# Prompt scores as two 128-row products with copied key parts, and half-wide cache tiles, in a two-layer streaming encoder step

## Chip, cores and metric

The kernel runs on one core of one Trainium2 chip. The metric is device time in microseconds (us) of one execution of the whole kernel. Before the change the median of three runs is 3021.28 us (3018.55 to 3021.63).

## What is computed

One step of a two-layer encoder over 1024 new tokens of one stream (the prompt) and 16 new tokens of each of eight running streams (the sample). Layer 0 mixes by stick-breaking attention (8 heads of 64) beside a convolution; layer 1 by banded attention (16 heads of 64) with a learned bias. Each layer ends in an MLP. The scores, which the change touches, are in the reference:

```python
def stick_breaking(q, k, v, q_pos, k_pos):
    z = jnp.einsum('bqhd,bkhd->bhqk', q, k) * (HEAD_DIM ** -0.5)
    mask = k_pos[None, :] < q_pos[:, None]
    log_keep = jnp.where(mask, jax.nn.log_sigmoid(-z), 0.0)
    between = lax.cumsum(log_keep, axis=3, reverse=True) - log_keep
    w = jnp.where(mask, jnp.exp(jax.nn.log_sigmoid(z) + between), 0.0)
    return jnp.einsum('bhqk,bkhd->bqhd', w, v)

def band_attention(q, k, v, q_pos, k_pos, rel_bias):
    s = jnp.einsum('bqhd,bkhd->bhqk', q, k) * (HEAD_DIM ** -0.5)
    ...
    p = jax.nn.softmax(jnp.where(mask, s, -jnp.inf), axis=-1)
    return jnp.einsum('bhqk,bkhd->bqhd', p, v)
```

## The kernel before

All dense products are made on TensorE in a reduced float32 type (F32R). To keep accuracy, a float32 operand is split into a high part (a copy in F32R, by ScalarE) and a low part (the rest, by VectorE), and a product takes three matmuls: high by high, high by low, low by high (`SPLIT`, L34; `split`, L173; `dense`, L205).

Activations lie transposed, features on the 128 partitions and tokens along the free axis. Heads go in pairs `p`: the head dimension is 64, so head 0 of a pair lies on partitions 0 to 63 and head 1 on 64 to 127. Layer 0 (`mixer0`, L544) has 4 pairs, layer 1 (`mixer1`, L991) has 8. For each pair the work is: projections of q, k and v of the *next* pair (`proj`, as filling), the spread of q and k into matmul operands (`expand_qk`), the scores of 8 query tiles of 128 per head (`attend`), stick-breaking or softmax on ScalarE and VectorE, transposes and the product with v (`weigh_steps`), and the sample's attention against cached keys and values (`sample_steps`).

How a score is made before the change:

- Layer 0: `qh`, `ql`, `kh`, `kl` are one tile each for both heads. A score block of up to 512 keys takes three matmuls on 64 rows (L820), and the last block of a query tile a fourth one on 128 rows that adds the mask (L822, `unit` by `maskd`).
- Layer 1: `qs` holds, for each head, the high part of q on the head's own 64 partitions and the low part on the other 64. `kd` holds the high part of k on both halves; the second half is filled by a copy DMA from SBUF to SBUF on the POOL queue (L1035). So one 128-row matmul gives (high + low of q) by high of k (L1101). The low part `kl` of k stands on the head's own partitions alone, and the second matmul is one of 64 rows (L1102). A query tile has one block up to 512 keys, and two (384 and 256) from the fifth tile on.

VectorE also makes the convolution of layer 0 (`tap`, L608): 31 multiply-adds over 1024 tokens for each of 4 channel groups, dealt out over the stages by `level` and `TAPS`. The sample's caches come through `load` in `sample_caches` (L423): tiles `ct` of 2048 columns (1 MB), two buffers, the next tile asked for when one is used. The DMAs for caches and weights stand on one queue (SP), and its wait for a free buffer holds back what is behind it.

The order of the work is set in three steps. `merge` (L50) deals lists of steps into one by their estimated TensorE time and the lags between dependent steps; `level` (L76) deals the taps among them; and the tile framework then fixes a static order for each engine, which may move an instruction past others. Engines wait for each other by semaphores and each works through its own queue in order.

Of the kernel before, what the change touches and what calls it, by code (L numbers as in the profile page):

```python
# [8 lines left out]
F32 = mybir.dt.float32  # L9
F32R = mybir.dt.float32r  # L10
# [27 lines left out]
def f(ap):  # L38
    return ap.bitcast(F32)
# [77 lines left out]
def tile_trunk(ctx, tc, ins, outs):  # L117
# [8 lines left out]
    def pool(name):  # L126
        return tc.tile_pool(name=name, bufs=1, reuse_waits="tile")
# [181 lines left out]


    class Cat:

# [92 lines left out]
    def sample_caches(layer, p, pl):  # L405


        name = f"{layer}{p}"
        srcs = {}
        for bg in range(2):  # L410
            if layer == 0:
                for c in range(2):
                    srcs["k", bg, c] = ins["sb_k"][p, bg * 4:bg * 4 + 4, :, c * 512:(c + 1) * 512]
            else:
                srcs["k", bg, 0] = ins["band_k"][p, bg * 2:bg * 2 + 2]
        for bg in range(2):
            for c in range(2 if layer == 0 else 1):
                srcs["v", bg, c] = ins["sb_v" if layer == 0 else "band_v"][p, bg, :, c * 2048:(c + 1) * 2048]
        order = list(srcs)
        at = {k: n for n, k in enumerate(order)}  # L420
        got = {}

        def load(kind, bg, n):  # L423
            i = at[kind, bg, n]
            for key in order[i:i + 2]:
                if key not in got:
                    got[key] = pl.tile([P, 2048], F32, tag="ct", name=f"ct{name}{key[0]}{key[1]}{key[2]}")
                    src = srcs[key]
                    if key[0] == "k":
                        src = src.rearrange("b p k -> p b k")  # L430
                        dma(got[key].rearrange("p (b k) -> p b k", b=src.shape[1]), src)
                    else:
                        dma(got[key], src)
            return got[kind, bg, n]

        return load

    def sample_steps(layer, p, bg, s, wk, load, soft, cs):

        nz = 2 if layer == 0 else 1
        name = f"{layer}{p}{bg}"
        qb = s["qb"]
# [8 lines left out]
        def keys(c):  # L453
            if c == 0:
                box["z"] = [bank(f"zs{name}{e}") for e in range(nz)]
            k = load("k", bg, c)
            for b in range(4):
                own = slice(32 * b, 32 * b + 32)
                mm(box["z"][c][own], qb[:, own], k[:, b * 512:b * 512 + 512], start=True, stop=True)  # L459

# [21 lines left out]
        def prod(k4):  # L482
            if k4 == 0:
                box["o"] = bank(f"so{name}")
                mm(box["o"][:, 0:P], wt["n"], s["vn"], start=True, stop=False)
            v = load("v", bg, k4)
            for j in range(4):
                for b in range(4):
                    own = slice(32 * b, 32 * b + 32)
                    c = j * P + 32 * b  # L490
                    mm(box["o"][own, 0:P], wt[k4][:, c:c + 32], v[:, (4 * j + b) * P:(4 * j + b + 1) * P], start=False,
                       stop=k4 == nz - 1 and j == 3)
# [9 lines left out]
        return ([Step(100.0, queries, 0.0, f"q{name}")]  # L502
                + [Step(1300.0, lambda c=c: keys(c), 0.0, None, f"q{name}", 3000) for c in range(nz)],
                [Step(215.0, new_keys, 2700.0 if layer == 0 else 1600.0, f"new{name}")],
# [39 lines left out]
    def mixer0():  # L544
        with ExitStack() as st:

            ep = Bufs(st.enter_context(pool("early0")), sg=3, kp=2)
            cp = Bufs(st.enter_context(pool("cache0")), ct=2)
            qb = ep.tile([P, P], F32, "qb", "qb0")
# [85 lines left out]
            def start():  # L635
# [21 lines left out]
                def ready(n, half):  # L657
                    src, t = st[n, half]
                    hl = None
                    if n > 1:  # L660
                        tag = ("qh", "ql", "kh", "kl")[2 * n - 4 + half]
# [113 lines left out]
            def expand_qk(p):  # L775
                q, k = S["sq", p], S["sk", p]
                ACT(qh, q[:, :TP], AF.Copy, scale=0.125)
                stt(ql, q[:, :TP], 0.125, f(qh), ALU.mult, ALU.subtract)
# [26 lines left out]
            def attend(p, cat):  # L805
                def job(i, t):
                    ws = {}
                    own = slice(64 * i, 64 * i + 64)

                    def one(q):  # L810
                        n = (q + 1) * P
                        w = ep.tile([P, TP], F32, "sg", f"sg{p}{i}{q}")
                        keep = ep.tile([P, TP + P], F32, "kp", f"kp{p}{i}{q}")
                        qs = slice(q * P, q * P + P)
                        for c in range(0, n, 512):
                            m = min(512, n - c)
                            z = bank(f"z{p}{i}{q}{c}")
                            last = c + m == n
                            for e, (a, b) in enumerate(((qh, kh), (qh, kl), (ql, kh))):
                                mm(z[:, :m], a[own, qs], b[own, c:c + m], start=e == 0, stop=e == 2 and not last)  # L820
                            if last:
                                mm(z[:, m - P:m], unit, maskd, start=False, stop=True)  # L822
# [9 lines left out]
                    def cost(q):  # L832
                        return 3 * max(256, q * P + P) * PASS

# [20 lines left out]
            start()  # L855
            qh, ql, kh, kl = (ep.tile([P, TP], F32R, n, n) for n in ("qh", "ql", "kh", "kl"))
            vs = pp.tile([P, 8, 2, 2, HD], F32R, "vs", "vs0")
# [133 lines left out]
    def mixer1(nx, win):  # L991
        h, rstd = nx.h, nx.r
        with ExitStack() as st:
# [35 lines left out]
            def expand_qk(p):  # L1029
                q, k = S["sq", p], S["sk", p]  # L1030
                for i in range(2):
                    own = slice(64 * i, 64 * i + 64)
                    oth = slice(64 - 64 * i, 128 - 64 * i)
                    ACT(kd[own, i], k[own, :TP], AF.Copy)
                    nc.gpsimd.dma_start(kd[oth, i], kd[own, i])  # L1035
                    ACT(qs[own, i], q[own, :TP], AF.Copy, scale=0.125)
                    stt(qs[oth, i], q[own, :TP], 0.125, f(qs[own, i]), ALU.mult, ALU.subtract)
                    tt(kl[own], k[own, :TP], f(kd[own, i]), ALU.subtract)
# [47 lines left out]
            def attend(p, cat):  # L1086
                def job(i, t):
                    ws = {}
                    own = slice(64 * i, 64 * i + 64)

                    def one(q):
# [6 lines left out]
                        for c, m in ((0, n),) if n <= 512 else ((0, 384), (384, 256)):  # L1098
                            z = bank(f"zc{p}{i}{q}{c}")
                            kc = slice(k0 + c, k0 + c + m)  # L1100
                            mm(z[:, :m], qs[:, i, qc], kd[:, i, kc], start=True, stop=False)  # L1101
                            mm(z[:, :m], qs[own, i, qc], kl[own, kc], start=False, stop=True)  # L1102
                            pieces.append((z[:, :m], S["bp", p, i][:, b0 + c:b0 + c + m], c, m))
# [357 lines left out]
```

## Time and profile before

| | us |
|---|---|
| median of three runs | 3021.28 |
| the profiled execution | 3022.33 |
| its span | 3020.5 |
| TensorE (PE) busy | 2958.1 |
| VectorE (DVE) busy | 2006.0 |
| ScalarE (ACT) busy | 1090.8 |
| mean granted TensorE clock, share of full | 0.987 |

The profile is of one execution. PE is matmuls, PEld loads of their stationary operand, which overlap matmuls. A matmul's recorded duration includes its way through the array, so that durations of neighbours overlap; what one costs in a stream is read from the distance between starts. In shapes such as `64*128 64x512`, the first pair is active rows by columns of the array, the second the moving operand. By time, layer 0's mixer takes some 90 to 600 us of the span, its output projection and MLP go on to about 1450, layer 1's mixer lies at about 1450 to 2135, and the rest is layer 1's output projection and MLP.

### The profile page before, as it was taken

Reading aid. Unit: us, or ns where it says so; the run is one execution under the profiler, and the core shown is the slowest. Engines: PE = TensorE matmul, PEld = TensorE weight load, DVE = VectorE, ACT = ScalarE, POOL = GpSimd, SP = SyncE. Lnnn points to the kernel's source line nnn. Section 1 sums busy time; section 2 is a strip of 40 time slices with the busy share of each in tenths; the row PEclk is TensorE's granted clock in tenths of the full one; section 3 lists DMA queues with packets and bytes.
Section 4 is the critical chain, followed back from the end, with each engine's and each line's share of the span. In section 5 each row is a group of like instructions: output and inputs, shape, how many; then the busy total and the mean of one; then the engine's idle time right before and its main releaser. Section 6 shows DMA issues by size and latency. Waiting matters only on the chain.

```text
span 3020.5 us, 45292 instructions
## 1 busy us (share of the span) xinstructions
PE 2958.1 (98%) x17786; PEld 2780.7 (92%) x17786; DVE 2006.0 (66%) x4021; ACT 1090.8 (36%) x2260; POOL 134.4 (4%) x293
## 2 busy tenths in 40 slices
PE   8999998999999999999999999999999999999998
PEld 8987786899999999999988888887999999999998
DVE  7998997865555555556666666667665555555556
ACT  5344446643222222222445444455442222222223
POOL 1000001000000000000101000100000000000001
PEclk9998998999999999999999999999999999999999
DMA  4333335331111111111433333335411111111101
GB/s 152 111 99 105 121 116 181 124 115 64 35 49 36 49 36 49 36 50 46 137 121 119 113 110 116 118 119 195 163 53 39 46 42 43 43 43 46 39 32 63
DMA packets 106677, 254.74 MB, mean 84 GB/s; under 512 B 17520, under 2 KB 22832, under 8 KB 102368
## 3 DMA queue, kind: packets, MB, share of 16 engines
q1 hardware_dynamic: 91728, 204.87, 20.4%
q0 software_dynamic: 14592, 46.97, 4.8%
q8 instruction: 139, 2.28, 0.3%
q14 instruction: 74, 0.61, 0.1%
q10 hardware_dynamic: 144, 0.02, 0.0%
HBM read 205.71 MB, written 41.84 MB: 82 GB/s over the span
## 4 chain that ended last, share of the span: by engine, by line
PE 85%; DVE 10%; ACT 3%; issue 1%; DMA 1%; DVEq 0%; SPq 0%; ACTq 0%
PE psu L214 26%; PE pd L1217 26%; PE psc L214 10%; PE psob L214 4%; PE psp L214 2%; DVE y L623 2%; PE psoa L214 2%; PE zc L1102 2%; PE avc L362 2%; DVE kp L801 2%; PE tpc L350 2%; PE zc L1101 1%; PE f L214 1%; PE zs L459 1%; PE z L820 1%
## 5 line engine op out<-in xcount | busy, mean ns | idle before, releaser
L214 PE MATMUL psu<-m,hl_wu 128*128 128x384 f32 x4608 | 808.3, 335 | 0.0
L1217 PE MATMUL pd<-hid,hl_wd 128*128 128x384 f32 x4608 | 807.4, 334 | 0.0
L214 PEld LDWEIGHTS psu<-m,hl_wu 128*128 128x128 f32 x4608 | 799.5, 188 | 1.6
L1217 PEld LDWEIGHTS pd<-hid,hl_wd 128*128 128x128 f32 x4608 | 799.5, 188 | 1.1
L1221 DVE TENSOR_TENSOR x<-x,pd 128x384 f32<-128x384 f32 x768 | 415.8, 550 | 194.6 <-PE pd L1217 191.8
L214 PE MATMUL psc<-h,hl_wc 128*128 128x384 f32 x1728 | 344.4, 345 | 0.0
L214 PEld LDWEIGHTS psc<-h,hl_wc 128*128 128x128 f32 x1728 | 293.5, 188 | 21.9 <-issue 15.0
L1201 DVE TENSOR_TENSOR s<-psu,rm 128x384 f32<-128x384 f32 x192 | 106.1, 555 | 282.7 <-PE psu L214 273.8
L175 ACT ACTIVATE hid<-s 128x384 fp32r<-128x384 f32 x192 | 100.7, 527 | 378.7 <-PE pd L1217 332.9
L175 ACT ACTIVATE hl_wd<-st_wd 128x512 fp32r<-128x512 f32 x128 | 80.6, 632 | 333.2 <-DMA st_wd<-in_w_down_dram 230.7
L1202 ACT ACTIVATE rl<-s 128x384 f32<-128x384 f32 x192 | 100.8, 525 | 215.1 <-DVE s L1201 211.4
L623 DVE SCALAR_TENSOR_TENSOR y<-u,dw,y 128x1024 f32<-128x1024 f32 (+1 forms) x232 | 177.1, 808 | 0.4
L214 PE MATMUL psp<-h,hl_wi 128*128 128x384 f32 x864 | 171.6, 345 | 1.5 <-DVE sk L767 1.5
L175 ACT ACTIVATE hl_wu<-st_wu 128x512 fp32r<-128x512 f32 x128 | 80.4, 628 | 226.2 <-PE psu L214 224.3
L176 DVE TENSOR_TENSOR hl_wu<-st_wu,hl_wu 128x512 fp32r<-128x512 f32 x128 | 88.5, 692 | 110.0 <-ACT hl_wu L175 107.2
L214 PEld LDWEIGHTS psp<-h,hl_wi 128*128 128x128 f32 x864 | 149.3, 191 | 4.6 <-issue 1.9
L176 DVE TENSOR_TENSOR hid<-s,hid 128x384 fp32r<-128x384 f32 x192 | 106.6, 555 | 68.9 <-ACT hid L175 68.8
L1203 DVE TENSOR_TENSOR s<-s,rl 128x384 f32<-128x384 f32 x192 | 106.2, 553 | 27.7 <-ACT rl L1202 24.4
L1067 ACT ACTIVATE s<-s,mxc 128x640 f32<-128x640 f32 (+4 forms) x128 | 88.8, 694 | 87.6 <-DVE mxc L1064 86.7
L1064 DVE CUSTOM_DVE_ANT_0 s<-zc,bp 128x384 f32<-128x384 f32 (+3 forms) x128 | 66.3, 518 | 53.6 <-PE zc L1102 52.4
L176 DVE TENSOR_TENSOR wlc<-tpc,whc 128x512 fp32r<-128x512 f32 (+1 forms) x144 | 82.3, 596 | 18.8 <-ACT whc L175 12.1
L176 DVE TENSOR_TENSOR hl_wd<-st_wd,hl_wd 128x512 fp32r<-128x512 f32 x128 | 87.4, 684 | 9.0 <-ACT hl_wd L175 8.7
(350 smaller groups left out, 3683.9 us busy)
## 6 DMA issues: line engine op xcount, KB each, us to landing
st_wu<-in_w_up_dram SPq DMA_DIRECT2D x128, 256.0 KB, 2.5
st_wd<-in_w_down_dram SPq DMA_DIRECT2D x128, 256.0 KB, 2.5
st_wc<-in_w_in_c_dram SPq DMA_DIRECT2D x48, 256.0 KB, 2.6
xm_d<-xo POOLq DMA_DIRECT2D x16, 576.0 KB, 3.6
x<-xm_d SPq DMA_DIRECT2D x16, 576.0 KB, 8.3
st_wi<-in_w_in_ab_dram SPq DMA_DIRECT2D x32, 256.0 KB, 3.2
cr<-cat_d SPq DMA_DIRECT2D x10, 576.0 KB, 3.9
bp<-in_bias_p_dram SPq DMA_DIRECT2D x16, 320.0 KB, 3.5
```

The source lines that it names most:

```text
L175: ACT(hi, src, AF.Copy)
L176: return tt(lo, src, f(hi), ALU.subtract)
L214: mm(ps()[:, :G], hl[:, a, at:at + P], act[g][k // 4][b][:, k % 4, :], start=n == 0, stop=n == len(todo) - 1)
L350: nc.tensor.transpose(tp[:, c0 + q * P:c0 + (q + 1) * P], blocks.get(j, tile_q), ident)
L623: stt(src if j == CW - 1 else dst, src, wj, dst, ALU.mult, ALU.add)
L1064: nc.vector.tensor_tensor_reduce(s[:, c:c + m], z, b, -1.0, mx, ALU.add, ALU.min, new)
L1067: ACT(s[:, :n], s[:, :n], AF.Exp, bias=mx, scale=-1.0, accum_out=tot)
L1201: tt(s, ps[:, :G], r[g], ALU.mult)
L1202: ACT(rl, s, AF.Relu)
L1203: tt(s, s, rl, ALU.mult)
L1217: mm(ps[:, :G], w[:, a, at:at + P], hid[2 * j + e, g][:, b], start=n == 0, stop=n == 5)
L1221: tt(xs, xs, ps[:, :G], ALU.add)
```

## The change

A new helper `expand` serves both layers. For each head of a pair it makes three tiles of 128 rows: `qs[i]` (high part of q on the head's own half, low part on the other), `kd[i]` (high part of k on both halves) and `kl[i]` (low part of k on both halves). Both second halves of k come by copy DMAs on the POOL queue. Each score block is then two matmuls of 128 rows in both layers; the product of the two low parts, which was left out in layer 0 and in the second matmul of layer 1, is now in the sum. Layer 0's cache tiles become 1024 columns wide with three buffers and the next two asked for ahead, so that the sample's keys come in 4 pieces of 256 and its values in 4 of 8 blocks. The reserve for the POOL queue's descriptors goes from 8192 to 4096 bytes a partition. `cost` in layer 0 counts two matmuls in place of three.

```diff
+    def expand(qs, kd, kl, q, k):
+        for i in range(2):
+            own = slice(64 * i, 64 * i + 64)
+            oth = slice(64 - 64 * i, 128 - 64 * i)
+            ACT(kd[i][own], k[own, :TP], AF.Copy)
+            nc.gpsimd.dma_start(kd[i][oth], kd[i][own])
+            ACT(qs[i][own], q[own, :TP], AF.Copy, scale=0.125)
+            tt(kl[i][own], k[own, :TP], f(kd[i][own]), ALU.subtract)
+            nc.gpsimd.dma_start(kl[i][oth], kl[i][own])
+            stt(qs[i][oth], q[own, :TP], 0.125, f(qs[i][own]), ALU.mult, ALU.subtract)
...
+        wide = 1024 if layer == 0 else 2048
...
-            for key in order[i:i + 2]:
+            for key in order[i:i + pl.bufs["ct"]]:
...
-                mm(box["z"][c][own], qb[:, own], k[:, b * 512:b * 512 + 512], start=True, stop=True)
+                mm(box["z"][at // 512][own, at % 512:at % 512 + kw], qb[:, own], k[:, b * kw:b * kw + kw],
+                   start=True, stop=True)
...
-            cp = Bufs(st.enter_context(pool("cache0")), ct=2)
+            cp = Bufs(st.enter_context(pool("cache0")), ct=3)
...
-                ACT(qh, q[:, :TP], AF.Copy, scale=0.125)
-                stt(ql, q[:, :TP], 0.125, f(qh), ALU.mult, ALU.subtract)
-                split(kh, kl, k[:, :TP])
+                expand(qs, kd, kl, q, k)
...
-                            for e, (a, b) in enumerate(((qh, kh), (qh, kl), (ql, kh))):
-                                mm(z[:, :m], a[own, qs], b[own, c:c + m], start=e == 0, stop=e == 2 and not last)
+                            mm(z[:, :m], qs[i][:, qc], kd[i][:, c:c + m], start=True, stop=False)
+                            mm(z[:, :m], qs[i][:, qc], kl[i][:, c:c + m], start=False, stop=not last)
...
-            qs = ep.tile([P, 2, TP], F32R, "qs", "qs1")
-            kd = ep.tile([P, 2, TP], F32R, "kd", "kd1")
-            kl = ep.tile([P, TP], F32R, "kl", "kl1")
+            qs, kd, kl = ([ep.tile([P, TP], F32R, f"{n}{i}", f"{n}{i}") for i in range(2)] for n in "qkl")
...
-                            mm(z[:, :m], qs[:, i, qc], kd[:, i, kc], start=True, stop=False)
-                            mm(z[:, :m], qs[own, i, qc], kl[own, kc], start=False, stop=True)
+                            mm(z[:, :m], qs[i][:, qc], kd[i][:, kc], start=True, stop=False)
+                            mm(z[:, :m], qs[i][:, qc], kl[i][:, kc], start=False, stop=True)
...
-    nc = bacc.Bacc("TRN2", target_bir_lowering=False, num_devices=1, dynamic_dma_scratch_size=8192)
+    nc = bacc.Bacc("TRN2", target_bir_lowering=False, num_devices=1, dynamic_dma_scratch_size=4096)
```

In the changed program the tiles of `qs`, `kd` and `kl` are named q, k and l with a number. The first place is TensorE in layer 0, the sixth query tile of a head in the first pair, with blocks of 512 and 256 keys. Before:

```order
L820 MATMUL z_1991<-kh,qh 128x512
L820 MATMUL z_1991<-kl,qh 128x512
L820 MATMUL z_1991<-kh,ql 128x512
L820 MATMUL z_1997<-kh,qh 128x256
L820 MATMUL z_1997<-kl,qh 128x256
L820 MATMUL z_1997<-kh,ql 128x256
L822 MATMUL z_1997<-maskd,unit 128x128
L214 MATMUL psp_1974<-h_210_592,hl_wi_1_1555 128x384
```

The same query tile, changed:

```order
L835 MATMUL z_2013<-k_738,q_736 128x512
L836 MATMUL z_2013<-l_740,q_736 128x512
L835 MATMUL z_2018<-k_738,q_736 128x256
L836 MATMUL z_2018<-l_740,q_736 128x256
L838 MATMUL z_2018<-maskd,unit 128x128
L214 MATMUL psp_1996<-h_210_592,hl_wi_1_1585 128x384
```

Two matmuls of six are gone, and the neighbours are as they were. The second place is TensorE in layer 1, a query tile with blocks of 384 and 256 keys, between a product with v (avc) and a projection of the next pair (psc). Before:

```order
L362 MATMUL avc_14779<-wlc_14746,vs_13793 128x128
L1101 MATMUL zc_14794<-kd_13791,qs_13790 128x384
L1102 MATMUL zc_14794<-kl_13792,qs_13790 128x384
L1101 MATMUL zc_14797<-kd_13791,qs_13790 128x256
L1102 MATMUL zc_14797<-kl_13792,qs_13790 128x256
L214 MATMUL psc_14766<-h_110_13528,hl_wc_1_14389 128x384
```

The same query tile, changed:

```order
L375 MATMUL avc_14850<-wlc_14817,vs_13862 128x128
L1107 MATMUL zc_14865<-k_13859,q_13857 128x384
L1108 MATMUL zc_14865<-l_13861,q_13857 128x384
L1107 MATMUL zc_14868<-k_13859,q_13857 128x256
L1108 MATMUL zc_14868<-l_13861,q_13857 128x256
L214 MATMUL psc_14837<-h_110_13594,hl_wc_1_14460 128x384
```

Count and order stay; the operands of the second matmul of each block now have 128 rows. The third place is the POOL queue in layer 0 where the second pair starts, in the changed program (cpa and cs are results on their way to the output projection, sk and sv the pair's k and v):

```order
L790 DMA out_sb_k_dram<-sk_1906 128x1152
L318 DMA k_737<-k_737 64x1024
L332 DMA cat_d_109<-cpa_2089 64x256
L318 DMA k_738<-k_738 64x1024
L790 DMA out_sb_v_dram<-sv_2150 128x1152
L645 DMA cat_d_109<-u_377 128x1024
L646 DMA cat_d_109<-u_377 128x8x16
L332 DMA cat_d_109<-cs_1917 128x128
L332 DMA cat_d_109<-cpa_2289 64x256
L321 DMA l_739<-l_739 64x1024
L321 DMA l_740<-l_740 64x1024
```

The four copies are new. Those of the low parts stand behind the write of cpa_2289, which waits for VectorE, and the first score of the pair needs l_739.

More of the change, by code (lines that the diff above doesn't have):

```diff
@@ L411, in sample_caches @@
             if layer == 0:
-                for c in range(2):
-                    srcs["k", bg, c] = ins["sb_k"][p, bg * 4:bg * 4 + 4, :, c * 512:(c + 1) * 512]
+                for c in range(4):
+                    srcs["k", bg, c] = ins["sb_k"][p, bg * 4:bg * 4 + 4, :, c * 256:(c + 1) * 256]
             else:
@@ L416, in sample_caches @@
         for bg in range(2):
-            for c in range(2 if layer == 0 else 1):
-                srcs["v", bg, c] = ins["sb_v" if layer == 0 else "band_v"][p, bg, :, c * 2048:(c + 1) * 2048]
+            for c in range(4 if layer == 0 else 1):
+                srcs["v", bg, c] = ins["sb_v" if layer == 0 else "band_v"][p, bg, :, c * wide:(c + 1) * wide]
         order = list(srcs)
@@ L424, in load @@
             i = at[kind, bg, n]
-            for key in order[i:i + 2]:
+            for key in order[i:i + pl.bufs["ct"]]:
                 if key not in got:
-                    got[key] = pl.tile([P, 2048], F32, tag="ct", name=f"ct{name}{key[0]}{key[1]}{key[2]}")
+                    got[key] = pl.tile([P, wide], F32, tag="ct", name=f"ct{name}{key[0]}{key[1]}{key[2]}")
                     src = srcs[key]
@@ L442, in sample_steps @@
         nz = 2 if layer == 0 else 1
+        nk, nv = (4, 2) if layer == 0 else (1, 4)
+        kw = 512 * nz // nk
         name = f"{layer}{p}{bg}"
@@ L456, in keys @@
             k = load("k", bg, c)
+            at = c * kw
             for b in range(4):
                 own = slice(32 * b, 32 * b + 32)
-                mm(box["z"][c][own], qb[:, own], k[:, b * 512:b * 512 + 512], start=True, stop=True)
+                mm(box["z"][at // 512][own, at % 512:at % 512 + kw], qb[:, own], k[:, b * kw:b * kw + kw],
+                   start=True, stop=True)
         def new_keys():
@@ L485, in prod @@
                 mm(box["o"][:, 0:P], wt["n"], s["vn"], start=True, stop=False)
-            v = load("v", bg, k4)
             for j in range(4):
+                v = load("v", bg, (4 * k4 + j) // nv)
                 for b in range(4):
@@ L490, in prod @@
                     c = j * P + 32 * b
-                    mm(box["o"][own, 0:P], wt[k4][:, c:c + 32], v[:, (4 * j + b) * P:(4 * j + b + 1) * P], start=False,
+                    at = (4 * (j % nv) + b) * P
+                    mm(box["o"][own, 0:P], wt[k4][:, c:c + 32], v[:, at:at + P], start=False,
                        stop=k4 == nz - 1 and j == 3)
@@ L502, in sample_steps @@
         return ([Step(100.0, queries, 0.0, f"q{name}")]
-                + [Step(1300.0, lambda c=c: keys(c), 0.0, None, f"q{name}", 3000) for c in range(nz)],
+                + [Step(1300.0 * nz / nk, lambda c=c: keys(c), 0.0, None, f"q{name}", 3000) for c in range(nk)],
                 [Step(215.0, new_keys, 2700.0 if layer == 0 else 1600.0, f"new{name}")],
@@ L660, in ready @@
                     if n > 1:
-                        tag = ("qh", "ql", "kh", "kl")[2 * n - 4 + half]
+                        tag = ("q0", "q1", "k0", "k1")[2 * n - 4 + half]
                         hl = ep.tile([P, TP], F32R, tag, f"hf{n}{half}").rearrange("p (a t) -> p a t", a=2)
@@ L807, in job @@
                     ws = {}
-                    own = slice(64 * i, 64 * i + 64)
                     def one(q):
@@ L813, in one @@
                         keep = ep.tile([P, TP + P], F32, "kp", f"kp{p}{i}{q}")
-                        qs = slice(q * P, q * P + P)
+                        qc = slice(q * P, q * P + P)
                         for c in range(0, n, 512):
@@ L832, in cost @@
                     def cost(q):
-                        return 3 * max(256, q * P + P) * PASS
+                        return 2 * max(256, q * P + P) * PASS
                     def dcost(q):
@@ L855, in mixer0 @@
             start()
-            qh, ql, kh, kl = (ep.tile([P, TP], F32R, n, n) for n in ("qh", "ql", "kh", "kl"))
+            qs, kd, kl = ([ep.tile([P, TP], F32R, f"{n}{i}", f"{n}{i}") for i in range(2)] for n in "qkl")
             vs = pp.tile([P, 8, 2, 2, HD], F32R, "vs", "vs0")
@@ L999, in mixer1 @@
             nc.gpsimd.memset(qb, 0.0)
-            qs = ep.tile([P, 2, TP], F32R, "qs", "qs1")
-            kd = ep.tile([P, 2, TP], F32R, "kd", "kd1")
-            kl = ep.tile([P, TP], F32R, "kl", "kl1")
+            qs, kd, kl = ([ep.tile([P, TP], F32R, f"{n}{i}", f"{n}{i}") for i in range(2)] for n in "qkl")
             vs = pp.tile([P, 8, 2, 2, HD], F32R, "vs", "vs1")
@@ L1030, in expand_qk @@
                 q, k = S["sq", p], S["sk", p]
[L1031 to L1038, printed above, removed]
+                expand(qs, kd, kl, q, k)
                 S["qn"] = pp.tile([P, P], F32, "qn", f"qn1{p}")
@@ L1088, in job @@
                     ws = {}
-                    own = slice(64 * i, 64 * i + 64)
                     def one(q):
```

## The prediction

> **What bounds the kernel now.** I read the page first, then the busy time by stretches of the two mixers, then the order of time on TensorE within them.
>
> ```profile
> span 3020.5 us, 45292 instructions
> ```
>
> ```profile
> 90.00:160.00 70.00, 70.00 (x440) 61.64 (x439) 66.75 (x87) 27.68 (x64) 3.79 (x7) 1.00 0.36 120
> 160.00:230.00 70.00, 64.85 (x456) 58.11 (x457) 69.38 (x98) 29.80 (x65) 4.98 (x9) 0.99 0.33 99
> 230.00:300.00 70.00, 67.76 (x397) 55.68 (x397) 61.80 (x87) 28.15 (x68) 3.99 (x8) 0.91 0.35 113
> 300.00:460.00 160.00, 147.79 (x1037) 125.52 (x1036) 157.88 (x224) 75.41 (x173) 17.11 (x29) 0.98 0.37 123
> 460.00:600.00 140.00, 124.97 (x763) 99.81 (x762) 116.34 (x214) 90.46 (x196) 9.21 (x17) 0.88 0.43 143
> 1505.00:2054.00 549.00, 542.97 (x3512) 460.83 (x3509) 367.43 (x1010) 270.42 (x614) 54.01 (x130) 1.00 0.37 118
> ```
>
> The columns are the stretch, its length, then busy us of PE, PEld, DVE, ACT and POOL, the granted clock and the DMA share. The two mixers have different limits. In layer 1 (last row, seven pairs) PE is busy 542.97 of 549 us at full clock, DVE 67%, ACT 49%. In layer 0 DVE is the fuller engine: 69.38 of 70 and 157.88 of 160, and it has slack only in the first, third and fifth row.
>
> ```profile
> PE tpc L350 <- DVE s L1069: 5.7, 7, 2.6
> ```
>
> This row of the waits of 1505 to 2054 is nearly all of what PE waits for there: 5.7 us. So time taken out of PE's own stream in layer 1 comes out of the kernel; in layer 0 it does so only where DVE has slack.
>
> Next, what a score costs PE in layer 1. The rows are start, duration, instruction, array rows by columns, moving shape, count; first the tiles q=2, q=3 and q=4 of a head, then what follows.
>
> ```profile
> 1747.68 0.42 PE L1101 MATMUL zc<-kd,qs 128*128 128x384 f32 x1
> 1748.03 0.44 PE L1102 MATMUL zc<-kl,qs 64*128 64x384 f32 x1
> 1748.40 5.47 PE L214 MATMUL psc<-h,hl_wc 128*128 128x384 f32 x30
> ...
> 1753.95 0.48 PE L1101 MATMUL zc<-kd,qs 128*128 128x512 f32 x1
> 1754.36 0.49 PE L1102 MATMUL zc<-kl,qs 64*128 64x512 f32 x1
> 1754.79 1.06 PE L459 MATMUL zs<-ct13k,qb 128*32 128x512 f32 x8
> ...
> 1757.37 0.39 PE L1101 MATMUL zc<-kd,qs 128*128 128x384 f32 x1
> 1757.69 0.44 PE L1102 MATMUL zc<-kl,qs 64*128 64x384 f32 x1
> 1758.06 0.38 PE L1101 MATMUL zc<-kd,qs 128*128 128x256 f32 x1
> 1758.37 0.38 PE L1102 MATMUL zc<-kl,qs 64*128 64x256 f32 x1
> ```
>
> ```profile
> 1758.68 2.38 PE L214 MATMUL psc<-h,hl_wc 128*128 128x384 f32 x12
> 1760.89 0.93 PE L350 MATMUL tpc<-ident,s 128*128 128x128 f32 x7
> 1761.58 0.42 PE L1101 MATMUL zc<-kd,qs 128*128 128x384 f32 x1
> ...
> 1765.04 0.40 PE L362 MATMUL avc<-wlc,vs 128*128 128x256 f32 x2
> 1765.28 0.34 PE L362 MATMUL avc<-whc,vs 128*128 128x256 f32 x2
> ```
>
> Among matmuls that all have 128 rows, 384 columns cost 0.173 us (the row below: 24.96 us for 144), 256 cost 0.12 (two in 1765.04 to 1765.28), 128 cost 0.10 (seven in 1760.89 to 1761.58). The score pairs cost far more: 0.72 us for two of 384 (1747.68 to 1748.40), 1.31 us for four (1757.37 to 1758.68).
>
> ```profile
> 1478.04 24.96 PE psc L214 x144
> ```
>
> The columns are the same, so the extra lies at the change from 128 rows to 64 and back, each time about 0.15 to 0.2 us. The psc behind loses some too: twelve take 1758.68 to 1760.89, 2.21 us, where 12 times 0.173 is 2.08; I take 0.1.
>
> Layer 0 shows that it is the change of row count and not the 64 rows:
>
> ```profile
> 195.63 0.34 PE L214 MATMUL psp<-h,hl_wi 128*128 128x384 f32 x1
> 195.90 0.49 PE L820 MATMUL z<-kh,qh 64*128 64x512 f32 x1
> 196.23 0.39 PE L820 MATMUL z<-kl,qh 64*128 64x512 f32 x1
> 196.46 0.39 PE L820 MATMUL z<-kh,ql 64*128 64x512 f32 x1
> 196.69 0.28 PE L820 MATMUL z<-kh,qh 64*128 64x256 f32 x1
> 196.81 0.28 PE L820 MATMUL z<-kl,qh 64*128 64x256 f32 x1
> 196.93 0.28 PE L820 MATMUL z<-kh,ql 64*128 64x256 f32 x1
> 197.14 0.33 PE L822 MATMUL z<-maskd,unit 128*128 128x128 f32 x1
> 197.30 1.26 PE L214 MATMUL psp<-h,hl_wi 128*128 128x384 f32 x6
> ```
>
> Inside the run of 64-row matmuls 512 columns cost 0.23 and 256 cost 0.12, as with 128 rows; only the first and the last of the run are dearer (0.33 and 0.21).
>
> **Layer 1, the scores.** After the change no row count alternates there. A tile of q=4 to 7 costs two times (0.173 + 0.12) = 0.59 in place of 1.31: 0.72 saved. q=2 saves 0.72 - 0.35 = 0.37, q=3 0.84 - 0.46 = 0.38; for the shorter q=0 and 1, 0.3 each. A head: 4 x 0.72 + 0.37 + 0.38 + 0.6 = 4.23; with 0.1 for each of some six returns, 4.83. 16 heads: 77 us. PE then needs about 9.7 us less of each pair's 78.4 (549 / 7); DVE's 52.5 and ACT's 38.6 a pair still fit into 69. What is late next is the wait of transposes for the softmax; I give back 8 us, somewhat over the 5.7 it costs now. Layer 1: -69. Bounds: the whole 77, or half of it.
>
> *Row tiling, the rule that speaks against the change.* The Trainium skill (TensorEngine Tiling (Array Packing), Theoretical Speedup) gives a product of at most 64 rows up to twice the speed, since two can lie in the array side by side; 128 copied rows give that up. The 64-row matmuls above follow each other at 0.23 us per 512 columns, so this kernel makes no use of it: they all lie on one head's half. Had the second matmul been free in that way, its own streaming time (per head 0.10 + 0.12 + 0.17 + 0.23 + 4 x 0.29 = 1.8 us, 29 us in 16 heads) would be given up, and the sum would come out near 2980 instead of 2951.
>
> **Layer 0, PE.** The tile above now takes 2 x (0.23 + 0.12) + 0.10 = 0.80 in place of 1.40, and the psp behind, 1.26 for six where five steps and a tail make 1.20, loses no 0.06: 0.66 saved, 0.35 of it the third products and 0.31 the change of rows. A head has 4608 columns, so third products are 9 x 0.23 = 2.1 us, 17 us in 8 heads; 64 tiles x 0.31 are 20. Against that, keys of the sample come in 32 groups in place of 16, each of which also changes the array's shape: 16 x 0.31 = 5. Net 32 us less for PE.
>
> **Layer 0, DVE.** Before, two operations of 128 partitions make the low parts of a pair; after, four of 64, and those are no shorter:
>
> ```profile
> L778 DVE SCALAR_TENSOR_TENSOR ql<-sq,qh x4: 1214/1217/1226, 91.5 to 457.3; 128x1024 fp32r<-128x1024 f32 x4
> ```
>
> ```profile
> L1038 DVE TENSOR_TENSOR kl<-sk,kd x16: 1209/1220/1224, 1492.9 to 2048.9; 64x1024 fp32r<-64x1024 f32 x16
> ```
>
> So 2 x 4 x 1.22 = 9.8 us more, on the engine that is full there: all of it counts. ACT's like amount has cover (28 to 90 busy per row above, under two thirds). DVE's idle time in the five rows is 3.3, 0.6, 8.2, 2.1 and 23.7: 37.9 us. PE's 32 us can shorten it only where PE is what DVE waits for: I take 3, 4 and 7 us in the first, third and fifth stretch, 14 in all.
>
> **Copies and loads.** A copy of this size is known from layer 1, and the wait ahead of it in the POOL queue from layer 0:
>
> ```profile
> DMA to landing us min/median/max: 3.2/5.0/6.3
> ```
>
> ```profile
> POOL cat_d L319 <- DVE cpa L372: 218.3, 19, 23.6
> ```
>
> ```profile
> ct01k<-in_sb_k_dram SPq DMA_DIRECT2D x4, 1024.0 KB, 5.2
> ```
>
> At the start of layer 0's second, third and fourth pair the low copy of head 0 stands behind a write that waits for cpa. From cpa to landing there pass the low part's 1.22 and 5.0, with issue some 7 us, at worst 9; PE has about as much in between (53 projection matmuls at the second pair, 9.2 us), less at the third and fourth. I take 1 us each, 3 in all; bounds 0 and 12. In layer 1 head 0's tiles are free half a pair earlier than now, and its copies start long before they are needed: nothing. The 16 added issues have an idle POOL as cover (54 of 549). Cache loads keep 1 MB ahead, now in halves of at most the 5.2 us above: nothing, at worst 1 us for each of the last pair's four keys.
>
> **The sum.** 3022.3 - 69 + 9.8 - 14 + 3 = 2952; the median lies 1 us below the profiled time: 2951.
>
> **Rivals.**
> 1. *Layer 0 follows PE.* If PE is what DVE waits for in its slack, up to 32 us go, limited by 37.9 - 9.8 = 28: with layer 1's 69 to 77 and no stall, 2916 to 2924. For it: PE is 70.00 of 70 in the first row. Against: 460 to 600 has both idle, at clock 0.88, so something else is late. Chance 0.17.
> 2. *Something else takes over in layer 1.* The softmax passes each tile from PE to DVE to ACT to DVE to PE; if its waits grow so that half of the 77 is kept, the sum is about 2982. Against: PE waits 5.7 us there now, and DVE would be at 76%. Chance 0.15.
> 3. *The copies stop PE.* PE works in order; if the first second-matmul of a pair waits for the low copy, everything behind waits. It happens at up to ten pair starts (3 and 7); to be slower than before, each must cost over 7 us, the whole way from cpa to landing with nothing beside it: 10 x 9 = 90 against 71 gives about 3040. Against: layer 1's copies start early. Chance 0.03.
> 4. *The extra is not the row count.* If the dear step belongs to the score pair itself, as to two products into one bank, layer 1 keeps its 77 us, and layer 0 gets only its 17 of third products, most of it where DVE is full: 3022 - 5 + 9.8 + 3, 3030. Against: the run of three products into one bank at 0.23. Chance 0.04.
>
> **How the numbers follow.** The forecast case, 2935 to 2970, has 0.61. The range goes to 2920, the middle of rival 1, and to 2985, just past rival 2; what is left out is the outer half of rival 1 and rivals 3 and 4, under 2 in 10. A measurement of this kernel can tell about 0.2%, 6 us. Faster by more: the forecast and rivals 1 and 2, 0.93; slower: rivals 3 and 4 without their edges, 0.05; between, 0.02.
>
> **What would show it.** Right: in layer 1, starts of the two score matmuls 0.17 us apart for 384 columns and psc right behind; the period of a pair near 69 to 70 us, PE still over 97% busy. In layer 0: two 128-row matmuls at 0.23 and a stage between 90 and 600 that is about as long as before, with DVE above 95% in its middle. Wrong: a period above 74, with PE waiting for DVE s or for kl's copy; score pairs still 0.35 apart; DVE's busy share in layer 0 falling while the stage grows.

## The result, and the profile after

The changed kernel takes 2948.85 us (median of 4 runs, 2948.08 to 2950.27); the kernel before takes 3021.13 us (median of 4, 3018.55 to 3021.63). The ratio is 0.9763 with a 95% interval of [0.9746, 0.978]: 72 us faster. The profiled execution took 2950.27 us, with this page:

```profile
span 2948.5 us, 45501 instructions
...
PE 2856.2 (97%) x17818; PEld 2746.9 (93%) x17818; DVE 2013.2 (68%) x4029; ACT 1095.1 (37%) x2268; POOL 150.7 (5%) x325
```

PE has 102 us less to do (2958.1 before), DVE 7 more (2006.0). Which stage got shorter is read best from the starts of the dense products, which line 214 makes for every stage. The view is that of one line of the code; at the end of each row's first part stand the first and the last start. Before:

```profile
L214 PE MATMUL psu<-m,hl_wu x4608: 334/334/628, 659.1 to 2980.9; 128*128 128x384 f32 x192
L214 PE MATMUL psc<-h,hl_wc x1728: 331/334/628, 1464.0 to 2045.2; 128*128 128x384 f32 x192
L214 PE MATMUL psp<-h,hl_wi x864: 331/334/668, 71.4 to 453.1; 128*128 128x384 f32 x173
L214 PE MATMUL psob<-cat,hl_wo0b x360: 333/336/442, 592.6 to 658.9; 128*128 128x384 f32 x180
...
L214 PE MATMUL psob<-cat,hl_wo1b x288: 334/336/423, 2151.7 to 2202.2; 128*128 128x384 f32 x144
```

The same rows of the changed kernel:

```profile
L214 PE MATMUL psu<-m,hl_wu x4608: 334/334/628, 649.5 to 2908.8; 128*128 128x384 f32 x192
L214 PE MATMUL psc<-h,hl_wc x1728: 331/334/628, 1454.4 to 1979.7; 128*128 128x384 f32 x192
L214 PE MATMUL psp<-h,hl_wi x864: 331/334/669, 68.3 to 445.8; 128*128 128x384 f32 x173
L214 PE MATMUL psob<-cat,hl_wo0b x360: 331/336/444, 584.2 to 649.3; 128*128 128x384 f32 x180
...
L214 PE MATMUL psob<-cat,hl_wo1b x288: 334/336/423, 2079.7 to 2130.1; 128*128 128x384 f32 x144
```

| stage, from the first start of one to that of the next | before | after | difference |
|---|---|---|---|
| up to the first psp | 71.4 | 68.3 | -3.1 |
| layer 0's mixer, psp to psob | 521.2 | 515.9 | -5.3 |
| output projection, psob to psu | 66.5 | 65.3 | -1.2 |
| MLP of layer 0, psu to psc | 804.9 | 804.9 | 0 |
| layer 1's mixer and output projection, psc to the last psob | 738.2 | 675.7 | -62.5 |
| the rest of the span | 818.3 | 818.4 | +0.1 |

Layer 1 gave 62.5 of the 72 us, layer 0 some 6.5. Each number is from one profiled execution: kernels below in which layer 0 has the same instructions as before take 518.1 to 523.9 us in its mixer, so some 3 us can be chance. The first 3 us are not the change's: no edit lies there, and executions of the kernels below have 66.5 to 70.3.

The busy time by stretches (stretch, length, then busy us of PE, PEld, DVE, ACT and POOL, granted clock, DMA share), as before the change:

```profile
90.00:160.00 70.00, 66.85 (x462) 60.09 (x461) 68.74 (x87) 30.71 (x70) 5.89 (x11) 1.00 0.48 146
160.00:230.00 70.00, 63.15 (x461) 57.33 (x461) 69.57 (x99) 30.39 (x65) 9.51 (x17) 0.98 0.39 108
230.00:300.00 70.00, 64.27 (x452) 53.84 (x452) 68.55 (x97) 31.71 (x75) 1.94 (x4) 1.00 0.39 112
300.00:460.00 160.00, 133.16 (x969) 114.92 (x968) 159.11 (x219) 76.63 (x170) 21.45 (x38) 0.94 0.44 133
460.00:590.00 130.00, 111.37 (x758) 92.12 (x759) 112.53 (x211) 87.96 (x192) 8.68 (x16) 0.92 0.50 165
1495.00:1989.00 494.00, 485.71 (x3513) 450.25 (x3512) 364.42 (x1011) 268.11 (x615) 60.92 (x144) 1.00 0.43 138
```

The last row is seven pairs of layer 1: 494 us in place of 549, PE still busy for 98% of them. In the rows of layer 0 PE fell well below its stretches, and DVE rose to 98 to 99% of the first four: DVE is now the fullest engine of layer 0 throughout.

The order of time on TensorE in layer 1, tiles q=2, q=3 and q=4 of a head (start, duration, instruction, array, moving shape, count):

```profile
1713.11 0.42 PE L1107 MATMUL zc<-k,q 128*128 128x384 f32 x1
1713.37 0.34 PE L1108 MATMUL zc<-l,q 128*128 128x384 f32 x1
1713.55 5.39 PE L214 MATMUL psc<-h,hl_wc 128*128 128x384 f32 x30
...
1719.02 0.48 PE L1107 MATMUL zc<-k,q 128*128 128x512 f32 x1
1719.34 0.40 PE L1108 MATMUL zc<-l,q 128*128 128x512 f32 x1
1719.66 1.07 PE L476 MATMUL zs<-ct13k,qb 128*32 128x512 f32 x8
...
1722.23 0.39 PE L1107 MATMUL zc<-k,q 128*128 128x384 f32 x1
1722.45 0.33 PE L1108 MATMUL zc<-l,q 128*128 128x384 f32 x1
1722.62 0.28 PE L1107 MATMUL zc<-k,q 128*128 128x256 f32 x1
1722.74 0.28 PE L1108 MATMUL zc<-l,q 128*128 128x256 f32 x1
1722.86 2.27 PE L214 MATMUL psc<-h,hl_wc 128*128 128x384 f32 x12
1724.97 0.93 PE L363 MATMUL tpc<-ident,s 128*128 128x128 f32 x7
1725.65 0.42 PE L1107 MATMUL zc<-k,q 128*128 128x384 f32 x1
1725.91 0.33 PE L1108 MATMUL zc<-l,q 128*128 128x384 f32 x1
```

The four of q=4 take 1722.23 to 1722.86, 0.63 us, where they took 1.31. Inside the four the steps are 0.17, 0.12 and 0.12, as forecast. But the first step of each tile is dearer than its columns: 0.22 behind avc (1722.23 to 1722.45), 0.26 behind the transposes tpc (1725.65 to 1725.91) and behind the sample's zn (1713.11 to 1713.37). And q=3 still takes 0.64 here, where the sample's keys zs, of another array shape (`128*32`), stand behind it; in the eight heads of this stretch in which psc stands behind it takes 0.55.

What PE waits for in the last row's stretch:

```profile
PE tpc L363 <- DVE s L1076: 5.3, 7, 2.2
```

That is about what it was before (5.7 us). In layer 0 the same view, from 80 to 590 us, shows where PE's time went. Before, and then after:

```profile
PE ava L362 <- DVE wla L176: 10.5, 9, 3.3
...
PE tpa L350 <- DVE sg L803: 3.3, 5, 1.5
```

```profile
PE ava L375 <- DVE wla L176: 19.1, 20, 3.7
PE tpa L363 <- DVE sg L820: 11.8, 14, 3.7
```

PE stands longer for the same two products of VectorE, 30.9 us in place of 13.8: about half of what it saved there is waited away. No row of these waits names a copy of k or l.

### The profile page after: what moved, and what is told of

Read it like the earlier page. It is cut to its first block, busy times and chain, and to the rows that moved or that the text cites. A ratio compares the mean times of both kernels' runs of the same rounds, so it can differ in the third digit from the quotient of the medians.

```text
span 2948.5 us, 45501 instructions
## 1 busy us (share of the span) xinstructions
PE 2856.2 (97%) x17818; PEld 2746.9 (93%) x17818; DVE 2013.2 (68%) x4029; ACT 1095.1 (37%) x2268; POOL 150.7 (5%) x325
## 4 chain that ended last, share of the span: by engine, by line
PE 82%; DVE 11%; ACT 3%; issue 2%; DMA 1%; POOL 0%; DVEq 0%; SPq 0%; ACTq 0%; POOLq 0%
PE psu L214 27%; PE pd L1223 27%; PE psc L214 10%; PE psob L214 4%; DVE y L642 3%; DVE kp L818 2%; PE avc L375 2%; PE psp L214 2%; PE psoa L214 2%; PE tpc L363 2%; PE f L214 1%; DVE sg L820 1%; PE zs L476 1%; PE zc L1107 1%; PE zc L1108 1%
```

## The experiments

Each kernel was timed against the kernel before on its own chip (3018.46 to 3018.71 us there; 3021.13 beside the change itself). A difference to the change's 2948.85 us can therefore be off by some 3 us, and the ratios are the safer comparison. The stage columns are read like those of the table above, from the kernel's one profiled execution.

| kernel | us | ratio to before, 95% | layer 0's mixer | layer 1's mixer and projection |
|---|---|---|---|---|
| layer 1 alone | 2956.06 | 0.9794 [0.9777, 0.981] | 523.9 | 673.0 |
| layer 1 alone, zeros for copies | 2958.19 | 0.9805 [0.9787, 0.9822] | 521.8 | 676.1 |
| layer 0 alone | 3012.72 | 0.9982 [0.9973, 0.9991] | 518.9 | 735.8 |
| cache tiles and reserve alone | 3014.03 | 0.9984 [0.9976, 0.9993] | 518.3 | 735.9 |
| cache tiles alone | 3015.24 | 0.9988 [0.9979, 0.9997] | 520.5 | 736.3 |
| reserve alone | 3017.40 | 0.9994 [0.9985, 1.0004] | 518.1 | 736.8 |
| changed, zeros for copies | 2948.04 | 0.9773 [0.9758, 0.9787] | 515.6 | 674.4 |
| changed, layer 0's second product on 64 rows | 2954.89 | 0.9791 [0.9778, 0.9805] | 521.6 | 677.1 |
| that, with wide cache tiles | 2956.74 | 0.9792 [0.9779, 0.9805] | 521.2 | 677.2 |
| changed, 9.8 us more on DVE in layer 0 | 2959.90 | 0.9803 [0.979, 0.9816] | 527.4 | 675.1 |
| zeros, layer 0's low k by GpSimd | 2956.62 | 0.9799 [0.9785, 0.9814] | 524.3 | 674.4 |
| zeros, sample's copies to ScalarE | 2942.32 | 0.9745 [0.9732, 0.9758] | 511.2 | 673.8 |

The theory: TensorE's extra in layer 1 was the change between 64 and 128 rows, and in layer 0 VectorE sets the time. The rivals are those of the prediction.

### Each layer alone

Layer 1 alone is the kernel before with `expand` and the two 128-row products in `mixer1` only:

```diff
-                            mm(z[:, :m], qs[own, i, qc], kl[own, kc], start=False, stop=True)
+                            mm(z[:, :m], qs[i][:, qc], kl[i][:, kc], start=False, stop=True)
```

> Only layer 1 is changed (both low parts of k copied, all score products on 128 rows); layer 0 and its cache tiles are as before. If layer 1's gain is TensorE time that the alternation of 64 and 128 rows took, and the two layers do not act on each other, the period of a pair in layer 1 goes from 78.8 to 70.8 us as in the changed kernel, and the time is about 62 us under before, near 2959. If instead layer 0's part reaches into layer 1 (through what is prefetched), it is under 50 us below before.

Layer 0 alone has the rest of the change, with the cache tiles and the reserve.

> Only layer 0 is changed (two products, copies, half-wide cache tiles, smaller descriptor reserve); layer 1 keeps its 64-row second product. The traces of before and after put layer 0's mixer about 7 us shorter and 3 us more at the very start. If the 3 us at the start belong to the spread between executions, this kernel is 5 to 8 us under before, near 3014; if they belong to the change, 10 us, near 3011. The prediction had about 1 us here, near 3020. Layer 1's period stays at 78.8.

Measured: 62.4 us less for layer 1 and 5.7 for layer 0, 68 together where the whole change gave 72. The two intervals allow some 5 us each way, so the parts add up as far as this can tell. Layer 1 carries the result.

### Is it the row count? Zeros in the other half

The kernel before, with layer 1's low k in a 128-row tile per head whose other half holds zeros, set once. No copy of the low part, no product of the two low parts: the same sum as before, on 128 rows.

```diff
+            for i in range(2):
+                nc.gpsimd.memset(f(kl[i][64 - 64 * i:128 - 64 * i]), 0.0)
...
-                            mm(z[:, :m], qs[own, i, qc], kl[own, kc], start=False, stop=True)
+                            mm(z[:, :m], qs[i][:, qc], kl[i][:, kc], start=False, stop=True)
```

> As before, but in layer 1 the low part of k lies in a tile of 128 rows per head whose other half is set to zero once, so the second product runs on 128 rows without a copy; it then sums the same terms as before. Layer 0 is as before. If the change of row count costs the time, this takes the same 62 us as the copies do, near 2959, period 70.8. If the dear step belongs to the pair of products into one bank, the period stays at 78.8 and the time near 3021.

It takes 2958.19 us, as layer 1 alone with its copies (2956.06). The order of time on TensorE of this kernel, tile q=2:

```profile
1718.41 0.42 PE L1106 MATMUL zc<-k,q 128*128 128x384 f32 x1
1718.67 0.34 PE L1107 MATMUL zc<-l,q 128*128 128x384 f32 x1
1718.85 5.39 PE L214 MATMUL psc<-h,hl_wc 128*128 128x384 f32 x30
```

The steps are those of the changed kernel, 0.26 and 0.18, 0.44 us for the tile. This kernel also gives each head tiles of its own, but TensorE waited for hardly anything in layer 1 before (5.7 us) and in the changed kernel (5.3), so little could be gained by that. So 60 us come from the row count alone, and rival 4 (the dear step belongs to the score pair itself) falls. The Trainium skill (TensorEngine Tiling (Array Packing), Key Properties) says that a change of tiling mode drains TensorE; these runs agree in that each change has a price: the four of a tile q=4 cost 1.31 - 0.63 = 0.68 us, 0.17 each.

### Are the copies covered? The changed kernel with zeros

The changed kernel without the copy of the low part, in both layers, with zeros as above. The product of the two low parts drops out of the sum again.

```diff
-            nc.gpsimd.dma_start(kl[i][oth], kl[i][own])
...
+            for i in range(2):
+                nc.gpsimd.memset(f(kl[i][64 - 64 * i:128 - 64 * i]), 0.0)
```

> The changed kernel without the copies of the low parts in either layer: the other half of each low tile is zero from the start on. The low-by-low term is then left out as it was before. If the copies are covered, as their landing times and the few waits for them say, the time is that of the changed kernel, 2949, within 2 us. If the low copies stop TensorE at pair starts (12 starts), it is 5 to 15 us less.

2948.04 against 2948.85 us, 515.6 against 515.9 in layer 0, and ratios of 0.9773 and 0.9763: no difference that these runs can tell; their intervals leave room for some 6 us. Rival 3, which needed over 70 us, falls. The forecast's 3 us are too small for the times to show; but no wait of TensorE in either mixer of the changed kernel names a copy.

### Layer 0: what PE's part is worth

The changed kernel with layer 0's second product on the head's own 64 rows, and no low copy there (the product of the two low parts is left out in layer 0):

```diff
-                            mm(z[:, :m], qs[i][:, qc], kl[i][:, c:c + m], start=False, stop=not last)
+                            mm(z[:, :m], qs[i][own, qc], kl[i][own, c:c + m], start=False, stop=not last)
```

> The changed kernel, but in layer 0 the second product of each block runs on the head's own 64 rows (no copy of the low part there), as layer 1 did it before: third products stay gone, the alternation of 64 and 128 rows comes back at each of 96 blocks, some 30 us more TensorE time than in the changed kernel. If TensorE's time counts in layer 0 as the result says (32 us less gave some 16), this is about 10 to 15 us slower than the changed kernel, near 2961. If layer 0 hangs on VectorE alone, it is within 3 us of it.

Its order of time on TensorE, the sixth query tile of a head:

```profile
192.22 0.40 PE L837 MATMUL z<-k,q 128*128 128x512 f32 x1
192.55 0.49 PE L838 MATMUL z<-l,q 64*128 64x512 f32 x1
192.97 0.38 PE L837 MATMUL z<-k,q 128*128 128x256 f32 x1
193.28 0.38 PE L838 MATMUL z<-l,q 64*128 64x256 f32 x1
193.60 0.33 PE L840 MATMUL z<-maskd,unit 128*128 128x128 f32 x1
193.76 1.26 PE L214 MATMUL psp<-h,hl_wi 128*128 128x384 f32 x6
```

Here the row count changes four times, and the tile takes 1.54 us. In the changed kernel it takes 0.76:

```profile
192.56 0.39 PE L835 MATMUL z<-k,q 128*128 128x512 f32 x1
...
193.26 0.22 PE L838 MATMUL z<-maskd,unit 128*128 128x128 f32 x1
193.32 1.26 PE L214 MATMUL psp<-h,hl_wi 128*128 128x384 f32 x6
```

The busy time over the whole of layer 0's mixer, from the first psp to the first psob (columns as in the stretches above), first of this kernel, then of the changed one:

```profile
67.30:588.90 521.60, 485.12 (x3190) 397.83 (x3189) 495.15 (x724) 258.93 (x569) 44.17 (x78) 0.96 0.41 127
```

```profile
68.30:584.20 515.90, 454.75 (x3189) 394.58 (x3188) 494.67 (x724) 257.29 (x569) 48.38 (x86) 0.96 0.43 132
```

PE has 30.4 us more to do, the 30 that were expected, and DVE the same. The mixer takes 5.7 us longer, the kernel 6.0 us, or 8 by the ratios (0.9791 against 0.9763, whose intervals allow 2 to 15): a fifth to under a third of PE's time shows, at most half, and the result lies between the two expectations. So layer 0 does not follow PE alone, and rival 1, by which all of it counts, falls.

### Layer 0: what DVE's part is worth

The changed kernel with the low part of q made twice in layer 0, eight operations more:

```diff
-            stt(qs[i][oth], q[own, :TP], 0.125, f(qs[i][own]), ALU.mult, ALU.subtract)
+            for _ in range(times):
+                stt(qs[i][oth], q[own, :TP], 0.125, f(qs[i][own]), ALU.mult, ALU.subtract)
```

> The changed kernel with the operation for q's low part done twice in layer 0 (same values): 8 more VectorE operations of 1.22 us, 9.8 us, nothing else. If all added VectorE time counts there, as the prediction has it, 9 to 10 us slower, near 2958; if the last stretch, where VectorE idles 17 us, hides a pair's share, 7; if it all hides beside TensorE, no change.

The view of tile q in this kernel, layer 0:

```profile
L323 DVE SCALAR_TENSOR_TENSOR q<-sq,q x16: 1215/1220/1221, 88.3 to 468.7; 64x1024 fp32r<-64x1024 f32 x16
```

Eight of these sixteen, 9.8 us, cost 11.1 us of the time (2959.90 against 2948.85), all of it in layer 0's mixer (527.4 against 515.9). In the changed kernel a microsecond on VectorE there is a microsecond of the time.

### The cache tiles and the reserve

The kernel before, with layer 0's cache tiles half as wide and the reserve at 4096:

```diff
+        wide = 1024 if layer == 0 else 2048
...
-            cp = Bufs(st.enter_context(pool("cache0")), ct=2)
+            cp = Bufs(st.enter_context(pool("cache0")), ct=3)
...
-    nc = bacc.Bacc("TRN2", target_bir_lowering=False, num_devices=1, dynamic_dma_scratch_size=8192)
+    nc = bacc.Bacc("TRN2", target_bir_lowering=False, num_devices=1, dynamic_dma_scratch_size=4096)
```

> The kernel before with the half-wide cache tiles of layer 0 (three buffers, two ahead) and the descriptor reserve of 4096 bytes alone; all scores as before. The prediction gave this part 5 us more of TensorE time (16 more changes of the array's shape) and put it on no path: 0 to 5 us slower than before. If the shorter prefetch makes TensorE wait for cache loads, over 5 us slower; if loads that stand behind cache loads on SP come earlier and that matters, faster.

Then the last line alone, and all but the last line:

> The kernel before with the reserve for DMA descriptors at 4096 in place of 8192, and nothing else. If the half-wide cache tiles gave the 4.5 us that tiles and reserve gave together (3014.03), this stays at 3018 to 3020, within 2 us of the kernel before. If the smaller reserve gave it, 3014.

> The kernel before with the half-wide cache tiles of layer 0 (three of them, each key and value part in two loads) and the reserve left at 8192. If the tiles gave the 4.5 us: 3014. If the reserve did: 3018 to 3020. If it takes both, because each added load needs descriptors: also 3018 or above.

Both together 4.5 us faster, the tiles alone 3.5, the reserve alone 1.3. The first two intervals exclude no change, the third includes it. So tiles and reserve together gave some 4 us (2 to 7 by the interval), most of it by the tiles as far as the medians go; what the reserve does is too small to tell. Layer 0 alone, which has both and the new scores beside, took 3012.72 us: the new scores by themselves are worth about 1 us there, less than the runs can tell. Where in layer 0 it is gained stays open: the profiled execution of the reserve alone, whose instructions stand in the order of before, has 518.1 us in the mixer too, against 521.2, so one profile of each doesn't place 3 us.

The same question beside the new scores: the kernel with the 64-row second product, one low tile for both heads, and the wide tiles.

> The changed kernel with layer 0's second product on 64 rows as before (that alone gave 2954.89), one low tile for both heads, and the wide cache tiles (two, of 2048 columns). If the half-wide tiles are worth the same 4 us beside the new scores as beside the old ones: 2959. If layer 0 is now so full on VectorE that a late cache load no longer ends last anywhere: 2955.

2956.74 against 2954.89 us, taken at different times, with ratios of 0.9792 and 0.9791: inconclusive, between both expectations.

This run shows more beside layer 1 alone (2956.06 us, ratio 0.9794): the two differ in layer 0's scores, with what feeds them, and in the reserve. Layer 0's mixer in the kernel before, and then in this one:

```profile
71.40:592.60 521.20, 487.24 (x3155) 412.96 (x3155) 483.47 (x713) 247.47 (x557) 39.98 (x70) 0.95 0.37 122
```

```profile
67.80:589.10 521.30, 486.28 (x3063) 396.32 (x3061) 494.86 (x724) 258.36 (x569) 44.13 (x78) 0.96 0.40 126
```

VectorE has 11.4 us more to do, TensorE as much as before, and neither the mixer nor the time is longer; the intervals of the two ratios leave room for some 6 us. So beside the old amount of TensorE work these VectorE operations cost little or nothing (unless the order of the steps, which the new `cost` deals anew, hid some of it; that was not tried apart), while in the changed kernel, with 30 us less on TensorE, 9.8 us cost 11.1. Before the change both engines were nearly as busy, 487.24 and 483.47 of 521.2 us.

### Two tries to relieve VectorE

First, layer 0's low k by GpSimd instead of VectorE (from the kernel with zeros, 2948.04):

```diff
-            tt(kl[i][own], k[own, :TP], f(kd[i][own]), ALU.subtract)
+            sub(kl[i][own], k[own, :TP], f(kd[i][own]), ALU.subtract)
...
+                expand(qs, kd, kl, q, k, nc.gpsimd.tensor_tensor)
```

> The kernel without low copies (zero halves), and in layer 0 the low part of k is made by GpSimd in place of VectorE: 8 operations, 9.8 us, off the full engine. If VectorE's time counts fully, 7 to 10 us less than the zero-half kernel, near 2940. Against it: GpSimd's queue then holds its copies and writes back behind work whose length no trace shows so far; if that delays the first scores of a pair, no gain or a loss of up to 10.

It is 8.6 us slower. The view of tile l of this kernel has the moved operation, the view of tile y the multiply-adds of the convolution on VectorE beside it:

```profile
L320 POOL TENSOR_TENSOR l<-sk,k x8: 2332/2894/3838, 94.8 to 461.1; 64x1024 fp32r<-64x1024 f32 x8
```

```profile
L641 DVE SCALAR_TENSOR_TENSOR y<-u,dw,y x218: 322/1265/2952, 61.8 to 445.4; 128x1024 f32<-128x1024 f32 x100, 128x128 f32<-128x128 f32 x9
```

The multiply-adds of the kernel with zeros, where VectorE makes the low k in 1.22 us:

```profile
L641 DVE SCALAR_TENSOR_TENSOR y<-u,dw,y x218: 323/1258/1286, 61.5 to 434.2; 128x1024 f32<-128x1024 f32 x102, 128x128 f32<-128x128 f32 x7
```

The longest multiply-add grows from 1.29 to 2.95 us: VectorE is held up beside the GpSimd operation. What all 218 take shows in the groups by line (busy us, then mean ns of one, then idle time), again of this kernel and of the one with zeros:

```profile
L641 DVE SCALAR_TENSOR_TENSOR y<-u,dw,y 128x1024 f32<-128x1024 f32 (+1 forms) x218 | 183.9, 892 | 0.1
```

```profile
L641 DVE SCALAR_TENSOR_TENSOR y<-u,dw,y 128x1024 f32<-128x1024 f32 (+1 forms) x218 | 172.4, 839 | 0.1
```

That is 11.5 us more, where eight operations of 1.22, 9.8 us, were taken off VectorE. Two more groups of the stick-breaking grew, the scans kp (86.0 to 88.2 us) and the products sg (47.6 to 49.2). In all VectorE is busy for 500.0 us of the mixer in place of 494.5, and idle for 24.3 in place of 21.1, which is the 8.7 us that the mixer is longer (524.3 against 515.6). The Trainium skill (SBUF — State Buffer, SBUF: two separate sides) says that VectorE operations with two inputs in SBUF and GpSimd operations hold one pair of ports in turn, each for its whole length; the 2.95 us agree with that.

Second, 16 copies in layer 0 from VectorE to ScalarE. They belong to the sample's attention output on its way out of PSUM; the expectation calls them copies of queries, which they are not:

```diff
-                nc.vector.tensor_copy(dst, tq[own, 0:P].rearrange("p (b h q) -> p b h q", h=2, q=16)[:, :, i])
+                src = tq[own, 0:P].rearrange("p (b h q) -> p b h q", h=2, q=16)[:, :, i]
+                if cat.layer == 0:
+                    ACT(dst, src, AF.Copy)
+                else:
+                    nc.vector.tensor_copy(dst, src)
```

> The changed kernel with zeros in the other half of the low keys and no copies (2948.04), and layer 0's copies of the sample's queries moved from VectorE to ScalarE: 16 operations of 0.22 us, 3.5 us. If every microsecond of VectorE in layer 0 counts, as the added 9.8 us did: 2945. If these copies lie where VectorE had slack, or ScalarE's queue now delays them: 2948 or above.

In the kernel with zeros the row of that line in layer 0 is:

```profile
L545 DVE COPY cs<-sq x16: 205/222/229, 186.8 to 583.9; 64x64 f32<-64x64 f32 x16
```

Without these 3.6 us the kernel takes 2942.32 us, 5.7 less than with zeros (2948.04) and 6.5 less than the change. It is the fastest of all; its five runs (2941.85 to 2945.56) lie below every run of those two, though they were not timed side by side. In the profiled executions layer 0's mixer is 4.4 us shorter (511.2 against 515.6). The direction is the theory's; why it gives more than the 3.6 us was not separated.

## Why the prediction was right, point by point

**The sum.** 2951 was forecast and 2948.85 came, but the terms were off and made up for each other: layer 1 gave 62.5 us where 69 stood, layer 0 some 6.5 where 1.2 stood, and 3.1 us at the start belong to no term. The way and the part of layer 1 were understood; that the sum came within 3 us is luck.

**Layer 1: mechanism right, size off.** The zeros show the mechanism. The term that was off is the 77 us gross. PE's busy time in seven pairs went from 542.97 to 485.71 us, which is 65 us in eight. The forecast took each new score at its columns' streaming time, 4.23 us saved a head, and 0.1 for each return. The first matmul of a tile is dearer than that (0.22 to 0.26 for 384 columns, not 0.173), and q=3 has the sample's keys behind it as before. From the trace after, a head's scores take 4 x 0.63 + 0.44 + 0.64 + 0.32 + 0.23 = 4.15 us (the last two are q=1 and q=0), where the forecast's terms leave 3.64 (4 x 0.59 + 0.35 + 0.46 + 0.47 for the shortest two). That is 0.51 a head and 8 us in 16 heads. Part of the extra that was put down to the row count belonged to the entry behind other work, and stayed. The other 4 us must lie at the returns: six psc behind q=0 took 1.15 us before and 1.12 after, less of a gain than 0.1. The 8 us given back were too many: PE's idle time in seven pairs went from 6.0 (549 - 542.97) to 8.3 (494 - 485.71), 2.6 us for eight. A pair took 494 / 7 = 70.6 us, against the 69 to 70 named as the sign.

**Rival 2** had as its condition that the softmax's waits grow until half is kept. The waits stayed at 5.3 us, and it fell.

**Layer 0, DVE: it counts after the change; beside the old PE work it did not show.** The forecast took DVE for the fuller engine, full in two of five stretches, and let all of its 9.8 us count. Over the whole mixer PE was as busy as DVE, and 11.4 us more on DVE beside that PE cost nothing that shows. In the changed kernel the same 9.8 us, added once more, cost 11.1.

**Layer 0, PE: its time right, its worth probably too high.** PE was to have 32 us less and had 32.5 (487.24 to 454.75). Of these, 14 were to come out of the time, by closing DVE's slack; the 30.4 us put back cost 6 to 8 (2 to 15 by the intervals). DVE's idle time in the mixer did fall by about the 14, from 37.7 (521.2 - 483.47) to 21.2 us (515.9 - 494.67), but with PE's 30.4 us put back it is still 521.6 - 495.15 = 26.5. So some 5 of these 16 us came from PE; the rest went with the cache tiles and with DVE's own added operations, which can fill idle time. The two terms together, 9.8 - 14, come to -4, and the new scores by themselves gave about 1 (3014.03 to 3012.72): both terms were too large in size, and their opposite signs kept the sum near.

**The copies: 3 us too many.** They were priced at 1 us for three pair starts; no wait of TensorE on a copy shows, and the kernel without them is as fast as far as the runs can tell.

**The cache loads: "nothing" failed.** Tiles and reserve gave some 4 us, and these are most of the difference between the 1.2 forecast in layer 0 and the 6.5 measured. The argument that 1 MB stays ahead either way looked at when data arrive; that the order or the loads beside it get better was not weighed, and the runs don't say which of them it is.

## What to carry to other kernels

Where matmuls of 64 and 128 rows alternate, fill the short ones up to 128 rows, with zeros if there is nothing better: the added rows stream for free (256 columns take 0.12 us within a run of 128-row matmuls, as they did within one of 64-row matmuls), and each change of row count cost 0.1 to 0.2 us here. Before such a gain is counted, find what sets the time of the stage: time saved on PE came out of the kernel nearly whole in layer 1, where PE was full, and by a fifth to under a third, as far as the runs tell, in layer 0. Where two engines are both nearly full, the worth of a microsecond on one depends on the other: 11.4 us more on VectorE cost nothing that shows beside the old PE work, and 9.8 us cost 11.1 once PE had been relieved. In the changed kernel an operation taken off VectorE paid in full, but not when the engine that took it over held VectorE up.

## What was not expected of the hardware

- The first matmul behind transposes or another kind of product costs some 0.05 to 0.09 us over its columns, though rows and array shape are the same (0.22 and 0.26 for 384 columns, where 0.17 is the step within a run).
- A subtraction of 64x1024 takes 1.22 us on VectorE and 2.33 to 3.84 on GpSimd beside a busy VectorE, and there it held up VectorE for longer than VectorE would have taken for it.
- In layer 0 a chain of 128, 64, 128, 64, 128 rows took 1.54 us where the same products on 128 rows took 0.76: twice the time for the same columns.
